# Moving six blocks' weight sums from GpSimd to VectorE, and the stores of the second-level forms behind the loads, in a Strassen-like MLP loop

## Chip, cores and metric

One core of a Trainium2 chip runs the whole program: TensorE (PE in the profile) multiplies, VectorE (DVE), ScalarE (ACT) and GpSimd (POOL) do elementwise work, and SyncE (SP) issues nearly all transfers between HBM and the on-chip memory. The metric is the device time of one execution in microseconds (us); lower is better. All data are float32.

## The reference, cut to what matters

The kernel computes one layer of a streaming encoder on 1024 tokens of width 1024: two groups of attention heads, cross-attention into 256 memory tokens, and a squared-ReLU MLP with 4096 hidden features, each with RMS norms around it. The change lies in the last part alone:

```python
h = rmsnorm(x, g_ff_pre[l])
y = jnp.square(jax.nn.relu(h @ w_ff1[l])) @ w_ff2[l]
x = x + rmsnorm(y, g_ff_post[l])
```

## The kernel before, in words

**Precision.** Each float32 operand of a product is split into a high part (a copy by ScalarE in a rounded format, `split_hi`) and a low part (operand minus high part, by VectorE, `split_lo`, L1848). A product is three matmuls: high by high, high by low, low by high (`mm3`, L193 to L195). A split therefore costs an activation and, behind it, one subtraction on VectorE.

**First MLP product.** `h @ w_ff1` is done by seven products per block in the manner of Strassen and Winograd instead of eight. The 4096 hidden features form 16 blocks (`NP` = 16) of two parts of 128. The loop `for j in range(NP)` at L2237 handles block j. Two of its seven products had been done ahead for the first seven blocks (`AHEAD` = 7) and lie in HBM; `reload(j)` (L2102) brings their two results back as one tile `p1r` of 512 KB. So iterations 0 to 6 have five products of 12 matmuls each, and the later ones have seven. The five, in order, with the PSUM bank that each adds to:

1. `px`, with the weight sums "s23";
2. `pz`, with "s1a";
3. `px` again, on top of the first, after VectorE has read `px` into `u2` (L2261);
4. `pv`, with "s1a";
5. `pz` again, with "s4", on top of the second product, after VectorE has read `pz` into `g22` (L2281).

Product 3 therefore waits for the addition `u2 = px + p1r`, and product 5 for the addition `g22 = pz + u3`, which itself needs `u3` (L2277, read from `px` after product 3).

**Weights.** `Weights(j)` loads two raw tiles of 512 KB (`load(0)`, `load(1)`, issue at L1833, three buffers in rotation). `sums` then makes three half-width sums (L2080 to L2082, 128x512) and `sum4` a fourth (L2087); both take an engine as argument and use GpSimd by default. Block 0's four are made on VectorE ahead of the loop (`cur.sums(nc.vector)`). All others are made on GpSimd at the head of iteration j for block j+1 (`nxt`). In the same iteration `nxt.split("s23")`, `split("s1a")` and `split("s4")` make the high and low parts. `load(1)` for block j+2 takes the buffer of raw tile 0 of block j+1, and so waits until `sum4` of that block has read it.

**What leaves VectorE.** At the head of iteration j `sums()` of the last iteration makes four results for block j-1 (L2316, L2318, L2320, L2322, written `s1`, `u2`, `s2`, `s4g`), and SyncE stores them (`put`, L1869). Where j is even, it also returns two forms (`put_sums`, L1893 to L1896: four VectorE instructions of 128x256 each, then two stores of 256 KB, L1898 and L1899). The first form is called right behind `g22`, the second at the end of the iteration, each with its stores at once.

**Order.** The order on every engine is the order in the program text (`manual_schedule`). SyncE's queue is in order too: a transfer that waits for its data holds all that are issued behind it.

Of the kernel before, what the change touches and what calls it, by code (L numbers as in the profile page):

```python
# [135 lines left out]
def build(ctx, tc, nc, out, t):  # L136
# [13 lines left out]
    def mm_tile(shape, name, tag="mm"):  # L150
        return psp.tile(shape, F32, tag=tag, bufs=2, name=name)
# [1646 lines left out]
    AHEAD = 7  # L1798
# [6 lines left out]
    def t2(name):  # L1805
        if region[0]:
            return pr.tile([P, HT], F32, tag="t2", bufs=9, name=name)
        return pf.tile([P, HT], F32, tag="t2", bufs=18, name=name)
# [3 lines left out]
    def bank(name, tag=None):  # L1812
        if tag is None:
            tag = ("mm", "s", "tr", "pv")[banks[0] % 4]
            banks[0] += 1
        return mm_tile([P, HT], name, tag)
# [38 lines left out]
    def product(ps, w, off, blk, more=False):  # L1855
        for kc in range(4):
            c = slice(off + kc * P, off + (kc + 1) * P)
            xh, xl = blk.at(kc)
            mm3(ps, w.hi[:, c], w.lo[:, c], xh, xl, kc == 0 and not more, kc == 3, more)
# [8 lines left out]
    def put(j, i, c):  # L1868
        nc.sync.dma_start(gd[i][j // 2][:, j % 2, :], c)  # L1869
# [19 lines left out]
    def put_sums(n, j, c):  # L1889

        k, s, e = j // 2 % 4, j // 8, even.pop(n)
        s12, s34 = t2(f"s12_{n}{j}"), t2(f"s34_{n}{j}")
        nc.vector.tensor_add(s12[:, :HQ], e[:, HQ:], c[:, HQ:])  # L1893
        nc.vector.tensor_sub(s12[:, HQ:], s12[:, :HQ], e[:, :HQ])
        nc.vector.tensor_sub(s34[:, :HQ], e[:, :HQ], e[:, HQ:])
        nc.vector.tensor_sub(s34[:, HQ:], c[:, :HQ], s12[:, HQ:])  # L1896
        return lambda: (
            nc.sync.dma_start(gi[n, ("S1", "S2")][s][:, :, k, :], s12.rearrange("p (a n) -> p a n", a=2)),  # L1898
            nc.sync.dma_start(gi[n, ("S3", "S4")][s][:, :, k, :], s34.rearrange("p (a n) -> p a n", a=2)))  # L1899
# [200 lines left out]
    def reload(j):  # L2100
        both = u4(f"p1r{j}", (P, 2, HT), F32)
        nc.sync.dma_start(both, p1d[j])  # L2102
        saved[j] = both[:, 0, :], both[:, 1, :]

    cur, nxt = Weights(0), Weights(1)
# [57 lines left out]
    def fetch(s):  # L2163

        n, k = steps[s]
        ra = wp.tile([P, D], F32, tag="wraw", bufs=3, name=f"ra{s}")
        rows_a[s] = ra
        if n in (("i", 0), ("i", 1)):
            name, h = inner[k // 2], k % 2
            nc.sync.dma_start(ra, gi[(1, 5)[n[1]], name][h].rearrange("p a b -> p (a b)"))  # L2170
            quads = {"A11": (0, 1), "A12": (2,), "S2": (3,), "S1": (), "S3": (0,), "S4": (3,), "A22": (2,)}[name]
            rows_b[s] = []
            for q in quads:
                rows_b[s].append(u4(f"wi{q}_{s}", (P, D), F32))
                nc.sync.dma_start(rows_b[s][-1], t["w_ff2q"][n[1], q, h])
            return
        i, name = order[n]
        nc.sync.dma_start(ra, gd[i][k].rearrange("p a b -> p (a b)"))
        if name == "T1":
            rows_b[s] = (raw_b(W12, k), raw_b(W11, k))  # L2180
        else:
            rows_b[s] = (raw_b({"B11": W11, "T2": W22, "T3": W11, "T4": W21}[name], k),)
# [50 lines left out]
        ops[s] = (ah, al, bh, bl)  # L2233

    with manual:
        sums = lambda: []
        for j in range(NP):  # L2237
            more = j + 1 < NP
            after = Weights(j + 2) if j + 2 < NP else None
            w = cur.w  # L2240
            if more:
                nxt.sums()
                nxt.sum4()
            if after:
                after.load(0)
            elif more:
                fetch(0)
            if j < AHEAD:
                p1, g11 = saved.pop(j)
                x = bank(f"px{j}")  # L2250
            else:
                x, _, g11, add = first_row(j, w["a"])
                add()
            if not more:
                fetch(1)
                fetch(2)
                prepare(0)
            product(x, w["s23"], 0, XT["T2"], more=j >= AHEAD)
            u2 = t2(f"u2_{j}")
            if j < AHEAD:  # L2260
                nc.vector.tensor_add(u2, x, p1)  # L2261
            else:
                nc.scalar.activation(u2, x, AF.Copy)
            forms = sums()
            relu2(g11)
            put(j, 0, g11)
            z = bank(f"pz{j}")
            product(z, w["s1a"], 0, XT["T1"])
            if more:
                if j + 1 >= AHEAD:  # L2270
                    nxt.split("a")
                if j:
                    nxt.split("s23")
            product(x, w["s23"], HT, XT["T3"], more=True)
            u3 = t2(f"u3_{j}")
            if j < AHEAD:
                nc.vector.tensor_add(u3, x, p1)  # L2277
            else:
                nc.scalar.activation(u3, x, AF.Copy)
            g22 = t2(f"g22_{j}")  # L2280
            nc.vector.tensor_add(g22, z, u3)  # L2281
            for form in forms[:1]:
                form()
            if more and not j:
                nxt.split("s23")
            if after:
                after.load(1)
            elif not more:
                prepare(1)
                fetch(3)  # L2290
            if j + 1 < AHEAD:
                reload(j + 1)
            v = bank(f"pv{j}")
            product(v, w["s1a"], HT, XT["T4"])
            if more:
                nxt.split("s1a")
            relu2(g22)
            put(j, 2, g22)
            nc.vector.tensor_sub(u3, u3, v)
            product(z, w["s4"], 0, XT["B22"], more=True)  # L2300
            if more:
                nxt.split("s4")
            relu2(u3)
            put_parts(1, j, u3)
            nc.vector.tensor_add(u2, z, u2)
            for form in forms[1:]:
                form()

            if not more:
                relu2(u2)  # L2310

            def sums(j=j, u2=u2, u3=u3, g11=g11, g22=g22):
                if j + 1 < NP:
                    relu2(u2)
                s1, s2, s4g = t2(f"s1_{j}"), t2(f"s2_{j}"), t2(f"s4_{j}")
                nc.vector.tensor_add(s1, u2, g22)  # L2316
                put(j, 3, s1)
                nc.vector.tensor_sub(u2, g11, u2)  # L2318
                put(j, 5, u2)
                nc.vector.tensor_sub(s2, s1, g11)  # L2320
                put(j, 4, s2)
                nc.vector.tensor_sub(s4g, u3, s2)  # L2322
                put_parts(5, j, s4g)
                return [lambda: put_sums(1, j, u3)(), lambda: put_sums(5, j, s4g)()] if j % 2 else []

            cur, nxt = nxt, after
        prepare(2)
# [141 lines left out]
        for s, (n, k) in enumerate(steps[:-3]):  # L2469
            if s and s < len(steps) - 2:  # L2470
                prepare(s + 2)
            for read in reads:
                read()
            del reads[:]
            if s == 1:
                forms = sums()
            if s in (2, 3):
                forms.pop()()
            if s == 4:
                pfs.close()  # L2480
            if s + 4 == len(steps):
                prepare(s + 3)
            if s + 4 < len(steps):
                fetch(s + 4)
            if isinstance(n, tuple):
                inner_multiply(s)
                if k % 2:
                    reads.append(lambda x=n[1], p=k // 2: inner_read(x, p))
                for call in later[:1]:
                    call()  # L2490
                del later[:1]
                continue
            if k == 0:
                if n == 0:
                    X = four(f"fx{n}", ("mm", "s"))
                elif n == 3:
                    Y = four(f"fy{n}", ("tr", "pv"))
            banks = Y if n == 3 else X
            multiply(banks, range(4), [s], n in (2, 4, 6))
            for call in later[:1 if n < 6 else 2]:  # L2500
                call()
            del later[:1 if n < 6 else 2]
            if n == 6 and k in (3, 4):
                residual(2 * k - 2)
                residual(2 * k - 1)
            if k == NK - 1:
                for tp in range(4):
                    gather(n, tp, banks[tp])
                finished(n)
# [75 lines left out]
```

## Time and profile before

| | us |
|---|---|
| median of three runs | 1463.97 |
| lowest and highest | 1461.88, 1464.31 |
| the profiled execution's own time | 1463.95 |
| its span, first to last instruction | 1462.1 |

The profile gives each engine's busy time, views of what ended each wait, and a timeline. Starts are microseconds from the start of the span. A matmul of 512 columns is listed at 0.39 us, but they overlap: their starts lie 0.227 us apart when nothing holds TensorE. So TensorE's lost time is read from the starts, or from the length of a stretch with known work, and not from its busy share. Iterations 0 to 6 of the loop at L2237 lie between 882.38 and 984.90 us.

### The profile page before, as it was taken

Reading aid. Unit: us, or ns where it says so; the run is one execution under the profiler, and the core shown is the slowest. Engines: PE = TensorE matmul, PEld = TensorE weight load, DVE = VectorE, ACT = ScalarE, POOL = GpSimd, SP = SyncE. Lnnn points to the kernel's source line nnn. Section 1 sums busy time; section 2 is a strip of 40 time slices with the busy share of each in tenths; the row PEclk is TensorE's granted clock in tenths of the full one; section 3 lists DMA queues with packets and bytes.
Section 4 is the critical chain, followed back from the end, with each engine's and each line's share of the span. In section 5 each row is a group of like instructions: output and inputs, shape, how many; then the busy total and the mean of one; then the engine's idle time right before and its main releaser. Section 6 shows DMA issues by size and latency. Waiting matters only on the chain.

```text
span 1462.1 us, 21876 instructions
## 1 busy us (share of the span) xinstructions
PE 1445.3 (99%) x7553; PEld 1232.0 (84%) x7553; DVE 1074.2 (73%) x1830; ACT 844.6 (58%) x1465; POOL 418.9 (29%) x520
## 2 busy tenths in 40 slices
PE   8999999999999999999999999999999999999998
PEld 8988888888889888888788888778888888888886
DVE  6777777767668847976873787785555776789897
ACT  6567677767677836555653455455555545555553
POOL 1245456545455301421321414333232000000003
PEclk9999999999999999999999999999999999999999
DMA  7132324321315595542531637775556897786885
GB/s 275 48 94 73 83 65 142 85 82 46 94 58 165 169 318 173 186 174 88 187 130 44 205 127 252 245 230 175 166 178 203 298 345 255 244 283 231 279 285 203
DMA packets 104351, 255.29 MB, mean 175 GB/s; under 512 B 11673, under 2 KB 30113, under 8 KB 104241
## 3 DMA queue, kind: packets, MB, share of 16 engines
q1 hardware_dynamic: 104096, 253.65, 52.6%
q8 instruction: 59, 0.97, 0.3%
q14 instruction: 52, 0.42, 0.1%
q10 hardware_dynamic: 144, 0.26, 0.1%
HBM read 184.07 MB, written 61.40 MB: 168 GB/s over the span
## 4 chain that ended last, share of the span: by engine, by line
PE 90%; DMA 3%; DVE 3%; issue 1%; ACT 1%; POOL 1%; SPq 0%; DVEq 0%; ACTq 0%
PE pv L754 4%; PE fx L194 4%; PE fx L193 4%; PE fx L195 4%; PE ptr L711 4%; PE px L194 3%; PE px L195 3%; PE px L193 3%; PE k L193 2%; PE q L193 2%; PE q L195 2%; PE q L194 2%; PE k L195 2%; PE k L194 2%; PE v L195 2%; PE v L193 2%
## 5 line engine op out<-in xcount | busy, mean ns | idle before, releaser
L717 DVE TENSOR_TENSOR phl<-ptr,phl 128x512 fp32r<-128x512 f32 (+1 forms) x152 | 92.5, 616 | 31.6 <-ACT phl L720 30.6
L720 ACT ACTIVATE phl<-ptr 128x512 fp32r<-128x512 f32 (+1 forms) x152 | 79.6, 539 | 40.3 <-PE ptr L711 38.5
L2357 POOL TENSOR_SCALAR rf<-sf 128x1 f32<-128x1 f32 x7 | 7.0, 1004 | 315.6 <-ACT jf L2338 315.4
L2229 ACT ACTIVATE whif<-ra 128x1024 fp32r<-128x1024 f32 x45 | 47.6, 1058 | 76.8 <-PE fx L194 34.7
L754 PE MATMUL pv<-phl,vs 128*128 128x512 f32 (+1 forms) x304 | 85.2, 366 | 0.2 <-DVE phl L717 0.2
L2231 DVE TENSOR_TENSOR wlof<-ra,whif 128x1024 fp32r<-128x1024 f32 x45 | 55.0, 1222 | 35.9 <-ACT whif L2229 35.8
L193 PE MATMUL fx<-vhif,whif 128*128 128x512 f32 x168 | 65.6, 391 | 0.0
L194 PE MATMUL fx<-vlof,whif 128*128 128x512 f32 x168 | 65.6, 391 | 0.0
L195 PE MATMUL fx<-vhif,wlof 128*128 128x512 f32 x168 | 65.4, 389 | 0.0
L754 PEld LDWEIGHTS pv<-phl,vs 128*128 128x128 f32 x304 | 55.2, 188 | 11.0 <-DVE phl L717 0.8
L2080 POOL TENSOR_TENSOR sc<-wf,wf 128x512 f32<-128x512 f32 x14 | 20.1, 1434 | 150.6 <-DMA wf<-in_w_ff 148.8
L768 POOL TENSOR_TENSOR o<-o 64x256 f32<-64x256 f32 x64 | 47.8, 747 | 52.7 <-DVE o L766 34.3
L766 DVE TENSOR_TENSOR o<-pv,o 64x512 f32<-64x512 f32 x64 | 44.0, 687 | 13.6 <-ACT o L771 12.2
L193 PE MATMUL k<-hT_hi,whik 128*128 128x512 f32 x128 | 53.6, 419 | 0.0
L193 PE MATMUL q<-hT_hi,whiq 128*128 128x512 f32 x128 | 51.6, 403 | 0.0
L193 PE MATMUL mq<-h2T_hi,whimq 128*128 128x512 f32 x128 | 51.4, 402 | 0.0
L195 PE MATMUL k<-hT_hi,wlok 128*128 128x512 f32 x128 | 50.4, 393 | 0.0
L193 PE MATMUL yw<-whiwo,yT_hi 128*128 128x512 f32 x128 | 50.3, 393 | 0.1
L195 PE MATMUL mq<-h2T_hi,wlomq 128*128 128x512 f32 x128 | 50.2, 392 | 0.2 <-DVE wlomq L455 0.2
L194 PE MATMUL k<-hT_lo,whik 128*128 128x512 f32 x128 | 50.3, 393 | 0.0
L195 PE MATMUL q<-hT_hi,wloq 128*128 128x512 f32 x128 | 50.2, 392 | 0.0
L194 PE MATMUL mq<-h2T_lo,whimq 128*128 128x512 f32 x128 | 50.2, 392 | 0.1
(715 smaller groups left out, 5214.6 us busy)
## 6 DMA issues: line engine op xcount, KB each, us to landing
wg<-in_w_ff SPq DMA_DIRECT2D x48, 512.0 KB, 6.2
ra<-gd SPq DMA_DIRECT2D x40, 512.0 KB, 4.4
wf<-in_w_ff SPq DMA_DIRECT2D x38, 512.0 KB, 4.5
wi<-in_w_ff2q SPq DMA_DIRECT2D x28, 512.0 KB, 5.5
wrawmq<-in_w_mq SPq DMA_DIRECT2D x16, 512.0 KB, 4.2
gd<-s SPq DMA_DIRECT2D x32, 256.0 KB, 2.1
gd<-g SPq DMA_DIRECT2D x25, 256.0 KB, 3.2
wrawq<-in_w_qk SPq DMA_DIRECT2D x8, 512.0 KB, 4.5
```

The source lines that it names most:

```text
L193: nc.tensor.matmul(ps, lh, rh, start=start, stop=False, skip_group_check=more)
L194: nc.tensor.matmul(ps, lh, rl, start=False, stop=False, skip_group_check=more)
L195: nc.tensor.matmul(ps, ll, rh, start=False, stop=stop, skip_group_check=more)
L711: nc.tensor.transpose(tr[:, m, :], sp[:, k * P:(k + 1) * P], ident)
L717: flow.put("V", at, 0.7, lambda: nc.vector.tensor_sub(pl[:, live, :], tr[:, live, :], f(ph[:, live, :])), done)
L720: flow.put("S", flow.end, 0.6, lambda ph=ph, tr=tr, live=live: nc.scalar.activation(ph[:, live, :], tr[:, live, :], AF.Copy), split)
L754: nc.tensor.matmul(pv[:, :, qs_, :], v, hl[:, :, hs, :], start=c == 0 and turn == 0, stop=last)
L766: flow.put("V", at, 0.7, lambda: nc.vector.tensor_add(o2[own], pv[own, :, :, ::step], o2[own]), lambda end: (free["pv"].give(end), flow.pu ...
L768: free["pv"].give(end), flow.put("G", end, 0.8, lambda: nc.gpsimd.tensor_add(o2[own, 0], o2[own, 0], o2[own, 1]), store)))
L2080: eng.tensor_sub(sc[:, k1], r0[:, k0], r1[:, k0])
L2229: nc.scalar.activation(ah, ra, AF.Copy)
L2231: nc.vector.tensor_sub(al, ra, f(ah))
```

## The change

In iterations 1 to 6 (`late`) the sums of the next block go to VectorE: the three of `sums` behind the issue of product 2 and ahead of `u3`, the fourth (`sum4`) behind `g22` and behind the first form. The split "s23" of the next block moves from the place ahead of `u3` to the place behind `sum4`. Iteration 0 and iterations 7 on keep GpSimd. In every iteration the forms' VectorE instructions stay where they are, but their stores are kept back: those of the first form until `load(1)` and `reload` have been issued, those of the second until `load(0)` of the next iteration has been issued. The short description speaks of seven blocks: the six of iterations 1 to 6, and block 0, which VectorE had already.

```diff
         sums, stores = (lambda: []), []
         for j in range(NP):
...
+            late = more and 0 < j < AHEAD
-            if more:
+            if more and not late:
                 nxt.sums()
                 nxt.sum4()
             if after:
                 after.load(0)
             elif more:
                 fetch(0)
+            for store in stores:
+                store()
...
             product(z, w["s1a"], 0, XT["T1"])
+            if late:
+                nxt.sums(nc.vector)
             if more:
                 if j + 1 >= AHEAD:
                     nxt.split("a")
-                if j:
+                if j and not late:
                     nxt.split("s23")
             product(x, w["s23"], HT, XT["T3"], more=True)
...
             nc.vector.tensor_add(g22, z, u3)
-            for form in forms[:1]:
-                form()
-            if more and not j:
+            stores = [form() for form in forms[:1]]
+            if late:
+                nxt.sum4(nc.vector)
+            if late or more and not j:
                 nxt.split("s23")
             if after:
                 after.load(1)
...
             if j + 1 < AHEAD:
                 reload(j + 1)
+            for store in stores:
+                store()
...
             nc.vector.tensor_add(u2, z, u2)
-            for form in forms[1:]:
-                form()
+            stores = [form() for form in forms[1:]]
...
-                return [lambda: put_sums(1, j, u3)(), lambda: put_sums(5, j, s4g)()] if j % 2 else []
+                return [lambda: put_sums(1, j, u3), lambda: put_sums(5, j, s4g)] if j % 2 else []
...
-                forms.pop()()
+                forms.pop()()()
```

More of the change, by code (lines that the diff above doesn't have):

```diff
@@ L2235, in build @@
     with manual:
-        sums = lambda: []
+        sums, stores = (lambda: []), []
         for j in range(NP):
```

## The prediction

> **What bounds the kernel now.** I read the page first.
>
> ```profile
> span 1462.1 us, 21876 instructions
> PE 1445.3 (99%) x7553; PEld 1232.0 (84%) x7553; DVE 1074.2 (73%) x1830; ACT 844.6 (58%) x1465; POOL 418.9 (29%) x520
> ```
>
> TensorE is busy for 99%, so any change off its path is worth nothing, and what can be won is where TensorE waits. The view of waits for TensorE, over the whole span, has these two at the place of the change:
>
> ```profile
> PE pz L193 <- DVE g L2281: 4.0, 2, 2.2
> ...
> PE px L193 <- DVE u L2261: 0.3, 1, 0.3
> ```
>
> Product 5 waited twice, 4.0 us in all, for the addition `g22`; product 3 once for `u2`. The cost is read better from stretches with equal work. I cut the loop at the first matmul of iterations 2 to 6 (columns: stretch, length, then busy time of PE, PEld, DVE, ACT, POOL with instructions, TensorE's granted clock, DMA share, GB/s):
>
> ```profile
> 909.58:923.18 13.60, 13.60 (x62) 11.27 (x60) 10.63 (x16) 6.70 (x10) 3.87 (x3) 1.00 0.62 199
> 923.18:941.10 17.92, 15.73 (x61) 12.26 (x60) 13.00 (x16) 8.17 (x13) 7.27 (x6) 0.90 0.82 280
> 941.10:954.70 13.60, 13.60 (x61) 11.27 (x60) 10.46 (x16) 6.69 (x10) 3.72 (x3) 1.00 0.59 192
> 954.70:971.07 16.37, 14.19 (x61) 11.11 (x60) 12.66 (x16) 8.07 (x13) 6.34 (x5) 1.00 0.84 290
> 971.07:984.90 13.83, 13.83 (x62) 11.19 (x60) 11.46 (x16) 7.16 (x11) 5.13 (x4) 1.00 0.56 190
> ```
>
> Sixty matmuls take 13.60 us undisturbed (0.227 each, 2.72 a product). Iteration 3 takes 4.32 more, iteration 5 takes 2.77 more, iteration 6 takes 0.23 more: **7.3 us is all that can be won**. In iteration 3 about 1.8 of the 4.32 are not the wait but the clock (0.90 over 17.92 us).
>
> Why is `g22` late in odd iterations? VectorE's timeline in iteration 5 (start, duration), and below it GpSimd's sums of block 6:
>
> ```profile
> 959.89 0.69 DVE L2261 TENSOR_TENSOR u<-px,p1r 128x512 f32<-128x512 f32 x1 [2.83 <-issue]
> ...
> 961.55 1.67 DVE L2318 TENSOR_TENSOR u<-p1r,u 128x512 f32<-128x512 f32 x1
> 963.15 1.78 DVE L2320 TENSOR_TENSOR s<-s,p1r 128x512 f32<-128x512 f32 x1
> ...
> 967.42 0.69 DVE L2281 TENSOR_TENSOR g<-pz,u 128x512 f32<-128x512 f32 x1
> ```
>
> ```profile
> 958.32 1.28 POOL L2080 TENSOR_TENSOR sc<-wf,wf 128x512 f32<-128x512 f32 x1 [13.35 <-DMA wf<-in_w_ff]
> ...
> 962.75 1.62 POOL L2087 TENSOR_TENSOR sd<-wf,sc 128x512 f32<-128x512 f32 x1
> ```
>
> Two things add up. `u2` starts 5.19 us into the iteration (959.89 less 954.70), though `px` is complete at about 2.9: it waits for `p1r`, as the row of ScalarE below shows. And while GpSimd works (958.32 to 964.37), VectorE's sums with two on-chip operands take 1.67 and 1.78 instead of 0.69. Iteration 2 shows that GpSimd is the cause: the sum that overlaps GpSimd's last takes 1.05, the next, after it, 0.69.
>
> ```profile
> 912.32 1.29 POOL L2087 TENSOR_TENSOR sd<-wf,sc 128x512 f32<-128x512 f32 x1
> ```
>
> ```profile
> 913.11 1.05 DVE L2316 TENSOR_TENSOR s<-u,g 128x512 f32<-128x512 f32 x1
> 914.19 0.69 DVE L2318 TENSOR_TENSOR u<-p1r,u 128x512 f32<-128x512 f32 x1
> ```
>
> **The change part by part.** I lay VectorE's new order out from T, the first matmul of an iteration, with steps from iteration 4 (T = 941.10) and from block 0's sums on VectorE.
>
> ```profile
> 944.02 0.69 DVE L2261 TENSOR_TENSOR u<-px,p1r 128x512 f32<-128x512 f32 x1 [2.03 <-PE px L195]
> ...
> 947.50 1.22 DVE L1848 TENSOR_TENSOR v1lo_s<-sc,v1hi_s 128x1024 fp32r<-128x1024 f32 x1
> 949.46 0.69 DVE L2277 TENSOR_TENSOR u<-px,p1r 128x512 f32<-128x512 f32 x1 [0.75 <-PE px L195]
> 950.19 0.69 DVE L2281 TENSOR_TENSOR g<-pz,u 128x512 f32<-128x512 f32 x1
> 950.80 0.42 DVE L1893 TENSOR_TENSOR s<-u,u 128x256 f32<-128x256 f32 x1
> 952.26 1.22 DVE L1848 TENSOR_TENSOR wlo_s1a<-wf,whi_s1a 128x1024 fp32r<-128x1024 f32 x1
> 953.40 0.68 DVE L2299 TENSOR_TENSOR u<-u,pv 128x512 f32<-128x512 f32 x1
> ```
>
> ```profile
> 877.02 0.68 DVE L2080 TENSOR_TENSOR sc<-wf,wf 128x512 f32<-128x512 f32 x1
> ...
> 879.19 0.69 DVE L2087 TENSOR_TENSOR sd<-wf,sc 128x512 f32<-128x512 f32 x1
> ```
>
> Start to start: `u2` and the four results 3.3 (3.48 in the row, 0.2 of it GpSimd's), three weight sums 2.2, `u3` 0.7, other 512-wide instructions 0.6, a low part of 1024 columns 1.14, a form 1.46.
>
> *Even iteration.* `u2` at T+2.9, the four results until 6.2, the new sums until 8.4. `u3` starts at 8.4 anyway (949.46), since product 3 ends there: **the three sums fit into a gap** and cost nothing as long as `u2` is in time; each 0.1 that it is late moves `g22` by 0.1. `g22` runs 9.1 to 9.8; product 5 wants it at 10.88 (four products). Then the form until 11.2, `sum4` until 11.85, the low part of "s23" 11.8 to 13.0; the next iteration wants it at 13.6. This margin was over 5 us (947.50 is T+6.4) and is now 0.6. Behind come "s1a" to 14.05, the `pv` subtraction 14.65, "s4" 15.25, `u2` 15.9, the second form 17.3: VectorE runs 3.7 us into the odd iteration. ScalarE's high part of "s23" needs only the three sums, so it is done before.
>
> *The transfers behind it.* SyncE's rows of iteration 4, the landing of `p1r` on ScalarE's row, and two landings from the DMA view (iterations 4 and 5):
>
> ```profile
> 951.70 0.52 SPq L1898 DMA_DIRECT2D gi1S<-s  x1
> ...
> 952.98 0.57 SPq L1833 DMA_DIRECT2D wf<-in_w_ff  x1
> 953.61 0.45 SPq L2102 DMA_DIRECT2D p1r<-p1d  x1
> ```
>
> ```profile
> 959.46 0.63 ACT L1865 ACTIVATE p1r<-p1r 128x512 f32<-128x512 f32 x1 [2.53 <-DMA p1r<-p1d]
> ```
>
> ```profile
> p1r<-p1d SPq DMA_DIRECT2D x1, 512.0 KB, 5.8
> ```
>
> ```profile
> p1r<-p1d SPq DMA_DIRECT2D x1, 512.0 KB, 4.6
> ```
>
> Before, `load(1)` left at T+11.9, behind two form stores. Now the stores are behind it, but it has a **new wait**: `sum4` must have read its buffer, which ends at 11.85. So it leaves no earlier; `reload` follows 0.63 later, at 12.5, and the stores behind both. Also behind the wait stand the stores of `g22` and of `u3`, which TensorE does not need. What the order gives is a faster landing: 5.8 with the stores in front (even), 4.6 without (odd). I take 4.6, since that row has the new order of neighbours, and keep 5.8 as the other end. `p1r` then lands 3.5 us into the odd iteration instead of 4.8. `load(0)` in front of the second form's stores is worth nothing by itself: nobody needs it before the next iteration. Those stores wait for the second form until 3.7 and hold up the store of the first result behind them, which is ready only at 5.0, so not at all. In an odd iteration `sum4` ends at 11.1 with `u2` at 3.7; `reload` goes at 11.8 and lands 2.8 us into the even one, in time for 2.9.
>
> *Odd iteration.* `u2` at 3.7 (VectorE's own backlog; `p1r` at 3.5), the four results 7.0, three sums 9.2, `u3`, then `g22` 9.9 to 10.6: in time for 10.88 by 0.3. There is no form, so VectorE is free at 15.3 and the next even iteration starts clean. With 5.8 `u2` comes at 4.7 to 5.1 (959.89 lies 0.43 behind the landing), `g22` ends at 11.6 to 12.0, and product 5 is 0.7 to 1.2 late.
>
> *VectorE's load.* Even 14.4, odd 11.5: 25.9 for a pair against TensorE's 27.2. It fits with 5% to spare.
>
> *Iteration 6* also makes the low part of block 7's "a" (1.14) ahead of `u3`: `g22` ends at 10.95, 0.1 to 0.2 late. GpSimd's 24 sums vanish from this stretch, and with them the slow VectorE rows. From iteration 7 on only the order of the form stores changes, where the first matmuls follow each other without a wait.
>
> *Sum.* 7.3 recovered, less 0.2 in each of iterations 3 and 5 for a margin of 0.3, less 0.2 in iteration 6: **6.7 us saved**. Span 1455.4; with the 1.85 around it 1457.25, against 1463.95 of the same execution, which is the median of the runs to 0.02.
>
> **The rivals.**
>
> *`p1r` no faster.* The landing stays at 5.8: 1.2 lost in iterations 3 and 5 each, and, since each late `sum4` delays the next reload, 0.8 in 6. 7.3 less 3.2 leaves 4.1: 1459.9. For it: `reload` leaves no earlier than before. Against: the 4.6 row. Still faster.
>
> *The clock.* The 1.8 us of iteration 3 might not come from its wait; then they stay, the saving is 4.9 and the time 1459.05. For it: the second wait, in iteration 5, left the clock at 1.00. Against: the slow clock stands in the stretch with the longest wait and in no other. The Trainium skill, page "TensorE: Matmul & The Clock Gate", section "What's actually happening", lets the clock fall after an idle window of about 3.4 us; by it a wait of 2.2 us need not have done this.
>
> *VectorE is the new bound.* If its steps in this mixture are 10 to 15% longer than in the rows, a pair takes 28.5 to 29.8 against 27.2, so 1.3 to 2.6 are lost per pair; three pairs give back 3.9 to 7.8 of the 7.3: about 1464. The small margins (0.3, 0.6) are for it; that rows of one shape repeat within 0.01 once GpSimd is quiet is against. The Trainium skill, page "Perfetto Trace Analysis", section "Optimizing Scalar/DVE Operations", says that work may go from a saturated VectorE to GpSimd, though a shared port can undo it; this change goes the other way, and its time by that rule is this rival's.
>
> *Slower.* The long VectorE rows come from the transfers (DMA share 0.82 and 0.84 in the two bad stretches, 0.59 and 0.62 in the good ones), not from GpSimd. Then they stay, and the moved sums are long as well: eight a pair at 1.78 instead of 0.72 are 8.5 more, a pair is 34.4, 7.2 over TensorE; three pairs lose 21.6, less the 7.3 of today: 1478. It becomes slower than before once the moved sums average about 1.2 (a pair of 29.6). Against: iteration 2's rows, at 0.69 as soon as GpSimd stops, and 953.40 at 0.68 just after two stores and a load were issued.
>
> **How the numbers follow.** The forecast has 0.64 (its own range 1456 to 1458.5), `p1r` no faster 0.16, the clock 0.03, VectorE as bound 0.11, slower 0.06. Faster by over 0.2% (2.9 us, about what a measurement of this kernel can tell from no change) are the first three, 0.83; within 0.2% is the fourth, 0.11; slower 0.06. The floor is 1456.65, with all 7.3 gone; single runs lie up to 2 us below their median, so the range starts at 1455.5. At the top it takes in the second and third case whole and the better part of the fourth, which begins at 7.3 less 3.9: 1462.5.
>
> **What would show it.** Right: stretches of iterations 1 to 6 of 13.6 to 14.0 us, no wait on `g22` above 0.5, L2316 to L2322 at 0.69 throughout, L2080 to L2087 on VectorE at 0.69, clock 1.00, `p1r` of even iterations landing in under 5. Wrong: waits on L2261 or L2281 in odd iterations near 1 us (`p1r`), a clock of 0.9 without a long wait (the clock), waits of product 1 on the low part of "s23" (VectorE as bound), or sums above 1.0 on VectorE with GpSimd idle (slower).

## The result, and the profile after

The changed kernel takes 1456.03 us in the median of six runs (1455.43 to 1458.34), beside 1463.98 of before (1460.82 to 1464.88) on the same chips: a ratio of 0.9953, with a 95% interval of 0.994 to 0.9966, or 5.0 to 8.8 us of gain. The profiled execution took 1455.46, with a span of 1453.7.

The page of after, then the view of TensorE's waits over the whole span (time in all, times, longest):

```profile
span 1453.7 us, 21860 instructions
...
PE 1443.0 (99%) x7553; PEld 1231.0 (85%) x7553; DVE 1093.1 (75%) x1854; ACT 845.1 (58%) x1465; POOL 389.1 (27%) x496
```

```profile
PE warm L1628 <- POOL ident masks.py:199: 1.3, 1, 1.3
PE v L194 <- DVE wlov L319: 0.6, 1, 0.6
```

The wait on `g22`, which led this view before with 4.0 us, is gone from it; what leads now is the start of the program. VectorE has 24 instructions more and GpSimd 24 fewer: six blocks of four sums. The stretches of iterations 2 to 6 (columns as before):

```profile
907.61:921.21 13.60, 13.60 (x61) 11.26 (x60) 11.32 (x19) 7.22 (x11) 0.00 (x0) 1.00 0.65 224
921.21:934.96 13.75, 13.75 (x62) 11.18 (x60) 13.26 (x22) 7.39 (x11) 0.00 (x0) 1.00 0.93 322
934.96:948.56 13.60, 13.60 (x62) 11.26 (x60) 11.69 (x20) 7.49 (x11) 0.00 (x0) 1.00 0.69 231
948.56:962.49 13.93, 13.86 (x61) 11.18 (x60) 13.61 (x22) 7.38 (x11) 0.00 (x0) 1.00 0.93 315
962.49:976.50 14.01, 13.88 (x62) 11.18 (x60) 12.34 (x20) 8.56 (x12) 0.00 (x0) 1.00 0.62 225
```

Iterations 3 and 5 went from 17.92 and 16.37 us to 13.75 and 13.93, and the clock of iteration 3 from 0.90 to 1.00. The seven iterations took 102.52 us (882.38 to 984.90) and take 96.09 (880.41 to 976.50): **6.4 us** are gained at the place of the change, with 0.9 left over the floor of 95.2. The spans differ by 8.4. The other 2.0 lie ahead of the loop, in code that is the same in both: the loop starts at 882.38 before and at 880.41 after, and in the trial kernels below anywhere from 880.67 to 882.43. From the end of iteration 6 to the end of the program both take 477.2, with 19.04 in each of iterations 7 to 15, so the new order of the stores there is worth nothing. So the 2.0 are the scatter of single executions and not the change, and the measured interval holds the 6.4.

VectorE in iteration 5 after the change, from `u2` to "s23":

```profile
952.80 0.69 DVE L2264 TENSOR_TENSOR u<-px,p1r 128x512 f32<-128x512 f32 x1
953.41 0.68 DVE L2323 TENSOR_TENSOR s<-u,g 128x512 f32<-128x512 f32 x1
...
956.06 0.68 DVE L2080 TENSOR_TENSOR sc<-wf,wf 128x512 f32<-128x512 f32 x1
...
958.11 0.68 DVE L2282 TENSOR_TENSOR u<-px,p1r 128x512 f32<-128x512 f32 x1
958.83 0.69 DVE L2286 TENSOR_TENSOR g<-pz,u 128x512 f32<-128x512 f32 x1
959.44 0.68 DVE L2087 TENSOR_TENSOR sd<-wf,sc 128x512 f32<-128x512 f32 x1
```

All rows are back at 0.69, the sums are at their new place, and `g22` ends at 959.52, 10.96 into the iteration; before it was 13.4.

### The profile page after: what moved, and what is told of

Same layout as the page of the kernel before. It is cut to its first block, busy times and chain, and to the rows that moved or that the text cites. A ratio compares the mean times of both kernels' runs of the same rounds, so it can differ in the third digit from the quotient of the medians.

```text
span 1453.7 us, 21860 instructions
## 1 busy us (share of the span) xinstructions
PE 1443.0 (99%) x7553; PEld 1231.0 (85%) x7553; DVE 1093.1 (75%) x1854; ACT 845.1 (58%) x1465; POOL 389.1 (27%) x496
## 4 chain that ended last, share of the span: by engine, by line
PE 96%; DVE 2%; ACT 1%; issue 0%; DMA 0%; SPq 0%; DVEq 0%; ACTq 0%
PE pv L754 4%; PE fx L194 4%; PE fx L193 4%; PE fx L195 4%; PE ptr L711 4%; PE px L195 3%; PE px L194 3%; PE px L193 3%; PE pz L193 2%; PE k L193 2%; PE mq L195 2%; PE q L193 2%; PE q L194 2%; PE q L195 2%; PE mq L194 2%; PE k L194 2%
## 5 line engine op out<-in xcount | busy, mean ns | idle before, releaser
L2080 POOL TENSOR_TENSOR sc<-wf,wf 128x512 f32<-128x512 f32 x8 | 12.7, 1589 | 176.9 <-DMA wf<-in_w_ff 163.3
L194 PE MATMUL q<-hT_lo,whiq 128*128 128x512 f32 x128 | 50.2, 392 | 0.0
```

Of the source, the lines that this page charges most:

```text
L194: nc.tensor.matmul(ps, lh, rl, start=False, stop=False, skip_group_check=more)
L2080: eng.tensor_sub(sc[:, k1], r0[:, k0], r1[:, k0])
```

## The experiments

The theory: TensorE's wait for `g22` in odd iterations had more than one cause, each long enough by itself: `p1r` landing late behind the forms' stores, GpSimd lengthening VectorE's rows, and the chain from `load(1)` over GpSimd's sums and the split of "s23" ahead of `u3`. The rivals: only one of these counts; or the long rows come from the transfers. T is again the first matmul of an iteration. Times are medians, and each ratio is against the kernel before on the same chip.

**Sums alone.** The sums stay on VectorE, the forms' stores leave at once.

```diff
-            stores = [form() for form in forms[:1]]
+            for form in forms[:1]:
+                form()()
...
-            stores = [form() for form in forms[1:]]
+            for form in forms[1:]:
+                form()()
```

> One part of the change alone: six blocks' sums on VectorE, but the forms' stores leave at once, so in even iterations they stand in front of load(1) and reload again. Theory (three things made g22 late: p1r behind the stores, GpSimd slowing VectorE, GpSimd's sums and the split ahead of u3): p1r leaves at T+12.5 as after the change but lands 5.8 later, so u2 of iterations 3 and 5 starts near T+4.9 and product 5 is about 1.2 us late there, 0.4 to 0.8 in iteration 6; seven iterations take 2.5 to 3.2 us more than undisturbed against 0.9 after the change; 1457.5 to 1459.5. Rival (VectorE is free of GpSimd, and that alone is the gain): the stretches are those of after, 1456.

1457.28 us, ratio 0.9962 (0.995 to 0.9975). Iterations 3 and 5 in the stretches, and SyncE's issues of iteration 4 (T = 936.13):

```profile
921.47:936.13 14.66, 14.16 (x62) 11.11 (x60) 13.24 (x22) 7.38 (x11) 0.00 (x0) 1.00 0.84 272
949.73:964.14 14.41, 14.01 (x61) 11.11 (x60) 13.24 (x22) 7.38 (x11) 0.00 (x0) 1.00 0.84 273
```

```profile
946.72 0.53 SPq L1898 DMA_DIRECT2D gi1S<-s  x1
...
948.00 0.57 SPq L1833 DMA_DIRECT2D wf<-in_w_ff  x1
948.63 0.44 SPq L2102 DMA_DIRECT2D p1r<-p1d  x1
```

The reload leaves at T+12.5, behind two stores, as before the change, and `u2` starts at 954.46, which is 4.73 into iteration 5. The seven iterations take 97.35, 1.26 more than after. This part alone gives 5.2 of the 6.4. The expected mechanism showed, but the sizes came out smaller: 2.15 us over the floor instead of 2.5 to 3.2, iterations 3 and 5 longer by 1.06 and 0.81 instead of 1.2, and a time 0.2 under the expected range. The rival (as after) did not hold.

**Stores alone.** The stores go behind the loads, all sums stay on GpSimd.

```diff
-            late = more and 0 < j < AHEAD
+            late = False
```

> The other part alone: the forms' stores behind the loads, all sums on GpSimd as before. Theory: load(1) of an even iteration no longer waits for a form, and its buffer is free early, so it leaves near T+8 instead of T+11.9 and p1r lands before the next iteration begins; GpSimd's sums move some 4 us earlier, so in odd iterations the split of s23 and the four results are done in time. Product 5 waits under 0.5 us in iterations 3 and 5, although VectorE rows above 1 us remain beside GpSimd: about 1456.5 to 1458. Rival (the slowing by GpSimd is what costs): iterations 3 and 5 keep waits of 2 us, 1462 to 1464.

1457.45 us, ratio 0.9962 (0.995 to 0.9975): also most of the gain. With the buffer free early, `load(1)` leaves iteration 4 at T+8.5, and `p1r` lands 0.85 us into iteration 5. The wait on `g22` is gone, as expected. But iterations 3 and 5 still take 14.65 and 14.61, since product 3 waits 0.7 us for `u2`, which was not expected. VectorE and GpSimd in iteration 5 show why:

```profile
953.66 1.41 DVE L1894 TENSOR_TENSOR s<-s,s 128x256 f32<-128x256 f32 x1
954.99 1.52 DVE L1895 TENSOR_TENSOR s<-s 128x256 f32<-128x256 f32 x1
...
956.76 0.68 DVE L2264 TENSOR_TENSOR u<-px,p1r 128x512 f32<-128x512 f32 x1
```

```profile
950.35 1.29 POOL L2080 TENSOR_TENSOR sc<-wf,wf 128x512 f32<-128x512 f32 x1 [7.41 <-DMA wf<-in_w_ff]
...
954.86 1.37 POOL L2087 TENSOR_TENSOR sd<-wf,sc 128x512 f32<-128x512 f32 x1
```

GpSimd's sums moved earlier and now lie beside the second form, whose 256-wide rows, 0.42 when GpSimd is quiet, take 1.41 and 1.52. So the slowing can cost at another place too, when it falls on a full VectorE (busy for 13.67 of the 14.61 us).

**The split ahead of `u3`.** After the change, with "s23" back at its old place.

```diff
-                if j and not late:
+                if j:
                     nxt.split("s23")
...
-            if late or more and not j:
+            if more and not j:
                 nxt.split("s23")
```

> After the change, with one step undone: the low part of s23 (1.14 us of VectorE) stands ahead of u3 again in iterations 1 to 6. Theory: it fits into no gap, since u3 follows the sums at once; g22 ends 1.1 later: even iterations 0.1 to 0.3 late, odd ones 1.0 to 1.5, iteration 6 about 1.4; 4 to 6 us of loss in seven iterations against 0.9; 1459 to 1461. Rival (its place does not matter, only the engine of the sums does): 1456.

1470.68 us, ratio 1.005 (1.0038 to 1.0063): slower than before, and three times the expected loss. TensorE's waits in the loop, VectorE in iteration 5, and that iteration's stretch:

```profile
PE pz L193 <- DVE g L2286: 10.3, 6, 2.8
```

```profile
968.09 0.69 DVE L2082 TENSOR_TENSOR sc<-wf,wf 128x512 f32<-128x512 f32 x1
969.96 1.22 DVE L1848 TENSOR_TENSOR v0lo_s<-sc,v0hi_s 128x1024 fp32r<-128x1024 f32 x1 [1.19 <-ACT v0hi_s L1845]
971.11 0.68 DVE L2282 TENSOR_TENSOR u<-px,p1r 128x512 f32<-128x512 f32 x1
```

```profile
958.61:977.07 18.46, 15.66 (x61) 12.28 (x60) 14.18 (x23) 8.74 (x13) 0.00 (x0) 0.91 0.81 271
```

I had counted the low part (1.14) and not that VectorE idles 1.19 in front of it, until ScalarE has made the high part from sums that VectorE has only just finished. So `u3` stands 2.3 us further behind the sums, except in iteration 6, where block 7's "a" fills the idle time. TensorE waits 1.1 to 1.3 us in iterations 1, 2, 4 and 6; in 3 and 5 the wait reaches 2.8 and the clock falls to 0.91. The place of the split is worth more than the whole gain.

**GpSimd kept busy.** After the change, with work on GpSimd that nobody needs.

```diff
+            if late:
+                junk = pw.tile([P, HT], F32, tag="gpjunk", bufs=1, name=f"gpjunk{j}")
+                for _ in range(4):
+                    nc.gpsimd.tensor_sub(junk, nxt.raw[0][:, k0], nxt.raw[1][:, k0])
```

> After the change, and GpSimd makes four more 128x512 subtractions of the same raw tiles in each of iterations 1 to 6, into a tile that nobody reads (work added, none left out). Theory (GpSimd's work is what lengthens VectorE's rows): rows of L2323 to L2329 and of the sums beside it go from 0.69 to 1.0 to 1.8, VectorE gets 2.4 to 3 us more per iteration, a pair of iterations needs about 31 us of VectorE against 27.2 of TensorE: product 5 waits in most iterations, 1465 to 1471. Rival (the rows are long because of the transfers, which this leaves as they are): rows stay at 0.69, 1456.

1472.33 us, ratio 1.0061 (1.0047 to 1.0074), a little above the expected range. GpSimd and VectorE in iteration 5:

```profile
961.38 5.78 POOL L2248 TENSOR_TENSOR gpjunk<-wf,wf 128x512 f32<-128x512 f32 x4 [11.42 <-DMA wf<-in_w_ff]
```

```profile
964.55 1.48 DVE L1896 TENSOR_TENSOR s<-s,s 128x256 f32<-128x256 f32 x1
965.95 0.68 DVE L2268 TENSOR_TENSOR u<-px,p1r 128x512 f32<-128x512 f32 x1
966.55 1.15 DVE L2327 TENSOR_TENSOR s<-u,g 128x512 f32<-128x512 f32 x1
967.74 0.69 DVE L2329 TENSOR_TENSOR u<-p1r,u 128x512 f32<-128x512 f32 x1
```

The long rows begin and end with GpSimd's work (to 967.16), and the edit adds no transfer. The rival that blamed the transfers falls, and the kernel after speaks against it as well: in its iterations 3 and 5 the DMA share was 0.93, above the 0.82 and 0.84 of before, with all rows at 0.69. The row at 965.95 lies in the midst of GpSimd's work and is not longer: it reads `px` in PSUM and only one operand in the on-chip memory that GpSimd uses too. In iterations 0 to 6 of the kernel before, 14 rows with an operand in PSUM ran beside GpSimd, and all took 0.68 or 0.69.

**Reload first, on the kernel before.** Only `reload` moves, behind `g22` and ahead of the first form's stores and of `load(1)`.

```diff
+            if j + 1 < AHEAD:
+                reload(j + 1)
             for form in forms[:1]:
                 form()
...
-            if j + 1 < AHEAD:
-                reload(j + 1)
             v = bank(f"pv{j}")
```

> The kernel before, with one transfer moved: reload is issued behind g22, ahead of the first form's stores and of load(1); the sums stay on GpSimd at their old times. Theory (p1r is only one of the causes): p1r leaves near T+8 and lands before the next iteration, u2 starts at 2.9; but GpSimd's sums of an odd iteration still run from 3.6 to about 9.7, s23's high part waits for them until 9, its low part ends near 10.2, and g22 near 11.6 to 12: product 5 is 0.8 to 1.2 late in iterations 3 and 5, the seven iterations take 97 to 97.8 us, 1458 to 1459.5. Rival (p1r behind the stores is the whole cause): no wait left, 95.4 us, 1456.5.

1465.1 us, ratio 1.0018 (1.0009 to 1.0026): no gain, slightly slower, so the expectation missed. `p1r` is in time and `u2` starts at T+2.9, yet iterations 3 and 5 take 15.48 and 15.82. What GpSimd does is enough by itself, as a link of the chain and by the rows that it lengthens; this run does not part the two. Iteration 5 (T = 954.39):

```profile
961.52 1.61 POOL L2082 TENSOR_TENSOR sc<-wf,wf 128x512 f32<-128x512 f32 x1
```

```profile
964.26 1.67 DVE L1848 TENSOR_TENSOR v0lo_s<-sc,v0hi_s 128x1024 fp32r<-128x1024 f32 x1 [0.58 <-ACT v0hi_s L1845]
...
966.57 0.69 DVE L2281 TENSOR_TENSOR g<-pz,u 128x512 f32<-128x512 f32 x1
```

The sums end at 963.1, the high part at 964.2, the low part at 965.9, `g22` at 967.3, which is T+12.9. I had put it at 11.6 to 12, with GpSimd's and VectorE's rows at their undisturbed lengths. And the edit has a cost of its own. In iteration 0 the reload's target buffer is in use until VectorE has split block 1's "s1a", and `load(1)` now stands behind it:

```profile
893.52 0.32 SPq L2102 DMA_DIRECT2D p1r<-p1d  x1
893.89 0.43 SPq L1833 DMA_DIRECT2D wf<-in_w_ff  x1
```

It left at 887.64 before. That makes iteration 1 take 15.96 us. A transfer moved to the front takes its wait along.

**All blocks on VectorE.** Iterations 7 to 14 too.

```diff
-            late = more and 0 < j < AHEAD
+            late = more and 0 < j
```

> After the change, with the sums of all later blocks (iterations 7 to 14) on VectorE as well. Theory (the gain is TensorE's waits alone, and there are none from iteration 7 on, where an iteration has 19.04 us of TensorE): iterations of 19.04 as before, 1456, no difference from after. Rival (GpSimd's slowing of VectorE costs in itself): a further gain of 1 us or more. Second rival (VectorE, with 2.8 us more per iteration and block a's low part ahead of u3, gets late there): waits on g22 or on the low part of s23 from iteration 7 on, 1457 to 1462.

1461.63 us, ratio 0.9993 (0.9984 to 1.0001): most of the gain is lost again; the second rival was right. Each of the eight later iterations loses 0.58 us (19.62 instead of 19.04 in the first), 4.7 in all. The part behind iteration 15 was 0.8 longer than after the change, but it was 0.8 and 1.1 longer in two of the trials above too (busy GpSimd, split ahead), so that is not laid to this edit. VectorE in iteration 7 here (T = 977.95) and, in the second fence, after the change (T = 976.50):

```profile
988.12 0.69 DVE L2323 TENSOR_TENSOR s<-u,g 128x512 f32<-128x512 f32 x1 [3.79 <-ACT u L1866]
...
993.98 0.68 DVE L2286 TENSOR_TENSOR g<-pz,u 128x512 f32<-128x512 f32 x1
```

```profile
991.61 0.68 DVE L2286 TENSOR_TENSOR g<-pz,u 128x512 f32<-128x512 f32 x1
```

Here the last block's results start only when ScalarE has squared `u2` behind its copy of `px`, so the three sums have no idle time to fall into, though VectorE is busy for only 14.57 of 19.62 us.

**What is left.** After the change, `reload` ahead of `load(1)`; and in a second kernel also block 7's "a" behind `sum4`.

```diff
+            if j + 1 < AHEAD:
+                reload(j + 1)
             if after:
                 after.load(1)
...
-            if j + 1 < AHEAD:
-                reload(j + 1)
             for store in stores:
```

> After the change, with reload issued ahead of load(1), so that p1r no longer waits for sum4. Theory (the 0.9 us that are left come from p1r in iterations 3 and 6 and from VectorE's backlog in iteration 5): p1r leaves near T+8 and lands early, u2 starts at 2.9 in even iterations and at 3.7 in odd ones; the loop's seven iterations take 95.4 to 95.7 us against 96.1; the time cannot be told from after, 1455.5 to 1456. Rival (VectorE's length alone sets what is left): 96.1 as after.

```diff
-                if j + 1 >= AHEAD:
+                if j + 1 >= AHEAD and not late:
                     nxt.split("a")
...
                 nxt.sum4(nc.vector)
+                if j + 1 >= AHEAD:
+                    nxt.split("a")
```

> As the run with reload ahead of load(1), and in iteration 6 the split of block 7's a moves behind sum4, so that its low part (1.14 us of VectorE) no longer stands ahead of u3. Theory: iteration 6 takes 13.6 us, seven iterations 95.2 to 95.4 us, which is the floor; 1455.3 to 1456. Rival (block 7's first product then waits for a's low part): iteration 6 or the first matmuls of iteration 7 lose 0.5 us or more.

1455.56 and 1455.75 us, ratios 0.9951 (0.9937 to 0.9964) and 0.9951 (0.9938 to 0.9963); neither can be told from after by its time. The first one's iterations 3, 5 and 6:

```profile
922.32:935.92 13.60, 13.60 (x61) 11.27 (x60) 13.39 (x22) 7.27 (x11) 0.00 (x0) 1.00 0.97 322
949.52:963.12 13.60, 13.60 (x61) 11.27 (x60) 13.39 (x22) 7.27 (x11) 0.00 (x0) 1.00 1.01 330
963.12:976.89 13.77, 13.77 (x62) 11.19 (x60) 12.12 (x20) 8.34 (x12) 0.00 (x0) 1.00 0.53 179
```

The seven iterations take 95.37 us against 96.09. In the second kernel iteration 6 takes 13.60 as well, and nothing is left to win in iterations 1 to 6; its iteration 0 lost 0.4, in code that both kernels share. But one execution is not enough to measure 0.7 us here. The kernel with all blocks on VectorE has the code of the kernel after in iterations 0 to 6, and took 95.52 for them. Its iterations 3 and 5:

```profile
923.23:936.97 13.74, 13.74 (x61) 11.18 (x60) 13.24 (x22) 7.39 (x11) 0.00 (x0) 1.00 0.94 319
950.57:964.17 13.60, 13.60 (x61) 11.26 (x60) 13.31 (x22) 7.39 (x11) 0.00 (x0) 1.00 0.95 321
```

The reload of iteration 3 took 4.8 us there and 5.2 after the change, and `u2` of iteration 4 started at T+2.98 and not at T+3.40, so VectorE came into iteration 5 in time. So the landing of `p1r` set most of what was left, but by how much changes from execution to execution; what both executions of this code lost and the earlier reload won back is only the 0.15 of iteration 3. The wait of iteration 0 that hurt the kernel before does no harm here, since VectorE makes the sums later than GpSimd did.

## Why the prediction was right

1457.25 was predicted and 1456.03 measured, on the forecast's own mechanism. The medians differ by 7.95 us, more than the 7.3 that could be won; that excess is put down to scatter, since the profiled executions differ by 6.4 in the loop and by 2.0 in the same code ahead of it. By its steps:

- *What can be won*: 7.3 us in iterations 3, 5 and 6. 6.4 were won there against 6.7 forecast; in the profiled execution the rest of the distance is the scatter ahead of the loop.
- *GpSimd's part*: shown by the trial with a busy GpSimd. Counted in the loop, ten of VectorE's 68 instructions of 512 columns took over 0.9 us before, and all ten overlap one of GpSimd; of those after, none did. One argument against the rival "slower" was weak: the row at 953.40 reads `pv` in PSUM, and such rows are not lengthened in any case. The rows at 0.69 beside a DMA share of 0.93, told with that trial, are the better argument.
- *The three sums in a gap*: right in even iterations, though the gap was made more than found. Before, in iteration 4, 0.75 us of it were VectorE's wait for product 3; the larger part, 1.14, was the low part of "s23", which the change moves behind `sum4`. The trial with the split at its old place shows what the sums cost without that. From iteration 7 on the same three sums delayed `g22`.
- *`load(1)` waits for `sum4`*: right. In iteration 4 `sum4` ends at 947.15, at T+12.19 and not at 11.85, since `u2` was late, and `load(1)` issues next:

```profile
946.47 0.68 DVE L2087 TENSOR_TENSOR sd<-wf,sc 128x512 f32<-128x512 f32 x1
```

```profile
947.18 0.33 SPq L1833 DMA_DIRECT2D wf<-in_w_ff  x1
947.56 0.42 SPq L2102 DMA_DIRECT2D p1r<-p1d  x1
948.04 0.52 SPq L1898 DMA_DIRECT2D gi1S<-s  x1
```

- *The landing of `p1r`*: mis-sized. 4.6 was taken, the two even iterations had 5.3 and 5.1, the odd ones 5.2 and 5.0. The sign that the prediction named, under 5 in even iterations, did not show; the rival's 5.8 did not either. The landing out of iteration 4, then `u2` of iterations 4 and 6, where it was to start at T+2.9:

```profile
p1r<-p1d SPq DMA_DIRECT2D x1, 512.0 KB, 5.1
```

```profile
938.36 0.69 DVE L2264 TENSOR_TENSOR u<-px,p1r 128x512 f32<-128x512 f32 x1 [1.70 <-DMA p1r<-p1d]
...
965.65 0.69 DVE L2264 TENSOR_TENSOR u<-px,p1r 128x512 f32<-128x512 f32 x1 [1.46 <-DMA p1r<-p1d]
```

  So `u2` of iteration 4 came at T+3.40, and VectorE carried that into iteration 5. There `u2` came at 4.2 and not at 3.7, and `g22` ended at 10.96 and not at 10.6; `u2` of iteration 6 came 0.24 late. That is why this execution has 0.9 left and not the forecast 0.6.
- *The clock*: 1.00 in every iteration of after. With the wait the slow clock of iteration 3 went too, and in the trials with a split ahead and a busy GpSimd it came back with long waits.
- *VectorE as bound*: not here, though it was busy for 13.61 of 13.93 us in iteration 5. The margin was real and thin: 2.3 us more ahead of `u3` made the kernel slower than before. The rival's own numbers, 7.3 less 3.9 to 7.8, give 1460.6 to 1464.5, so neither "about 1464" nor a case that begins at 1462.5; the forecast does not rest on that.
- *What the working did not see*: the causes were alternatives in part. Each half of the change alone gave about 5 us (7.3 less 2.15 and 2.35 left over), and not a share of the sum; by its trace the stores' half worked mainly because `load(1)`, freed of the form, left 3 to 4 us earlier, which the full change gives up again for `sum4`.

## What to carry to other kernels

Where TensorE waits for one addition on VectorE, list everything that stands ahead of it in VectorE's order, and what each waits for; a chain over two engines (sum, high part, low part) costs its wait as well as its instructions. Two-operand work on GpSimd is not free for a full VectorE: it lengthened VectorE's rows with two on-chip operands by up to 1.1 us each, before the change and in both trials that moved or added such work. And a gap that takes added work in one iteration has to be looked for anew in the next kind of iteration.

## What the runs showed of the hardware

- VectorE instructions with both operands in the on-chip memory took up to 1.78 us instead of 0.69 (512 columns) and up to 1.52 instead of 0.42 (256 columns) beside GpSimd, and those with an operand in PSUM kept their 0.69. The Trainium skill, page "GPSIMD Engine Reference", section "8. Key points", names this contention; the factors, up to 2.6 and 3.6, are from these runs.
- The granted clock was 0.90 to 0.92 in iterations with one wait of TensorE of 2.2 to 2.8 us (before, the split ahead, the busy GpSimd), and 0.91 in iteration 3 of the busy GpSimd, with two waits of 1.9. It stayed at 1.00 in iterations whose longest wait was 1.6 to 2.1 (iteration 5 of before, reload first). So the length of a single wait does not decide alone; what else does is not shown. The Trainium skill, page "TensorE: Matmul & The Clock Gate", section "What's actually happening", gives an idle window of about 3.4 us for the fall. Every one of these waits was shorter; the measurement decides.
